# A decoder layer whose branch and output projections take seven block products for eight, in one stream of units with the MLP

## The chip, the cores and the metric

The kernel runs on 1 core of one Trainium2 chip. The metric is the device time in microseconds, the median of three runs. Everything is computed in float32; a product of two float32 matrices is made of three passes on TensorE (below), and the kernel is written in a tile language that places the semaphores and orders the instructions of each engine by a plan of its own, except where the code fixes their order.

## What is computed

One layer: a mixer with three branches, gates, an output projection with a residual, and a squared-ReLU MLP with a residual. D is 1024, the sequence 1024, the MLP's width 4096. The reference, cut to what matters here:

```python
h = rms_norm(x, norm_mix_g)
proj = h @ w_in                        # q, k, v and gates of three branches
y_m = ...                              # mLSTM, 4 heads (branch M)
y_d = ...                              # differential attention, 8 heads (branch D)
y_c = ...                              # cross attention into 256 memory tokens (branch C)
g_m, g_d, g_c = split(sigmoid(h @ w_gate + b_gate), 3)
merged = g_m * (y_m @ w_proj_m) + g_d * (y_d @ w_proj_d) + g_c * (y_c @ w_proj_c)
x = x + merged @ w_out
h2 = rms_norm(x, norm_mlp_g)
x = x + square(relu(h2 @ w_up)) @ w_down
```

## The kernel before, in words

**Three passes.** Each float32 operand is split into a high part (a cast to fp32r, on ScalarE, ACT) and a low part (the difference, on VectorE, DVE): `split2` and `split`, L102 to L115. `mm3` (L117, its matmuls are L91) then multiplies high by high, high by low and low by high into one PSUM bank. Activations lie feature-major: 128 features on the partitions, 1024 positions along the free dimension, cut in two halves of 512.

**Stages.** `run` (L1616) goes through: the norm and transposition of x; branch C; branch M; 64 positions of gate products; branch D; 96 positions of gate products; then `tail`. A position is one `yield` of a generator, mostly three matmuls of 128x512. In branches M and C, `weave` (L476) runs a stream of such positions and fires helper steps at listed positions; in branch D `fill` (L975) draws positions between the steps of attention. The branch outputs y and the gates go to DRAM.

**The tail before.** `tail` (L1297) takes the branches in the order C, M, D. For each, `k_tiles` (L1263) loads the eight y tiles from DRAM and splits them; `load_w` loads and splits the weights of 256 output columns; `group` computes two output tiles by two halves, eight blocks of k each, three passes: 8 x 8 blocks x 2 halves x 3 matmuls a projection. `merge` (L1339) multiplies the PSUM result with the gate fetched from DRAM and adds the three branches; the sum over the third branch is split at once into the operands of the output projection (`hi` and `lo`, which stay in SBUF). The output projection is a `group` of the same kind, with `res` (L1357) as its end: residual, store of x1, a square for the norm, a scaled copy h2, stored to DRAM.

**The MLP before** already works with seven products for eight (Winograd's form of Strassen's scheme): a unit is a quad of 2 x 2 blocks of 128 output features by two halves; a step is one pair of k blocks, seven products of three matmuls (21 matmuls of 128x512); a unit of the up projection has four steps and seven PSUM banks, which rotate over the eight. Four sums of weight blocks (`wino_s`, L1142, on GpSimd, POOL) and four of x blocks (`wino_t`, L1123, three on DVE and one on POOL) make the operands, which are then split; `combine` (L1193) makes four output tiles from the seven banks by seven DVE adds and one ACT copy. `wino` (L1174) begins with the first unit cut in two runs of two steps and its partial sums parked in SBUF, while the remaining x tiles arrive. The norm of the MLP (`rstd`, L1411) is folded in behind the up products: a matmul with ones sums the squares, POOL takes the power -1/2, DVE scales eight identity blocks, and TensorE broadcasts them. `use_up` (L1397) scales, applies ReLU and square, and writes r to DRAM with its four sums. `down` (L1445) makes 16 passes of four steps with 28 accumulators in SBUF; its x tiles come from DRAM and are split again.

**Order.** The MLP and the branches pin the order of TensorE and DVE to that of the program (`InOrder`, L57, and `pin`, L86); ACT, POOL and the DMA queue of SyncE (SP) are ordered by the planner. An engine works its queue strictly in order, so an instruction that waits holds up what stands behind it.

## Time and profile before

| | |
|---|---|
| median of 3 runs | 2211.47 us (2211.36 to 2213.92) |
| profiled execution | 2213.57 us, span 2211.8 us, granted clock 0.995 |
| TensorE busy (matmul) | 2163.4 us, 98% of the span |
| DVE, ACT, POOL busy | 1361.4, 980.7, 527.8 us |
| DMA | 273.06 MB, mean 123 GB/s |
| first and last matmul on kt (branch projections) | start at 1218.5 and 1482.2 us |
| first matmuls of the up and of the down part | 1575.2 and 1891.8 us |

How to read it: the span runs from the first to the last instruction on the core. A row of a group gives line, engine, operation, output and inputs with their shape, the count, then the busy time in us, the mean duration in ns, and the idle time of the engine just before with what ended it. A row of a stretch gives begin and end, its length, and for each engine the busy time with the count of instructions, then TensorE's granted clock, the share of DMA time and GB/s. Matmuls overlap in the pipeline, so the mean duration of one is more than its share of time.

### The profile page before, as it was taken

The page shows a single profiled execution, that of the slowest core. Times are in us where ns is not written, and L with a number is a line of the kernel's source. Part 1 is how long each engine was busy: PE and PEld are TensorE (multiplying, and loading weights), DVE is VectorE, ACT ScalarE, POOL GpSimd, SP SyncE. Part 2 cuts the span into 40 slices and gives each one's busy share as a digit, 9 for nine tenths or more (in the row PEclk, how much of TensorE's full clock was granted, in tenths as well). Part 3 has the DMA queues.
Part 4 walks back from the last instruction along what each step waited for, and adds up shares of the span by engine and source line. Part 5 has one row for each costly group of instructions (what it writes and reads, how often), then busy time and mean ns, then how long its engine had stood idle before and what let it go on. Part 6 is the DMA issues. An engine that isn't in the chain of part 4 may idle for free.

```text
span 2211.8 us, 30588 instructions
## 1 busy us (share of the span) xinstructions
PE 2163.4 (98%) x11097; PEld 1860.7 (84%) x11097; DVE 1361.4 (62%) x2598; ACT 980.7 (44%) x1962; POOL 527.8 (24%) x696
## 2 busy tenths in 40 slices
PE   7999999999999999999999999999999999899999
PEld 5878888898899999999888888877787888688887
DVE  6643575565237777777641232544688877767779
ACT  6543355454336666666542120223444444543332
POOL 2100000000011111111000003202557655565553
PEclk9999999999999999999999999999999999999999
DMA  7023122121333333333343443436435444854444
GB/s 250 29 81 115 50 91 76 44 82 39 107 109 86 93 84 84 88 92 86 101 148 114 134 142 126 138 110 205 147 115 198 159 147 147 318 196 146 145 145 170
DMA packets 127948, 273.06 MB, mean 123 GB/s; under 512 B 12945, under 2 KB 21430, under 8 KB 125750
## 3 DMA queue, kind: packets, MB, share of 16 engines
q1 hardware_dynamic: 125494, 258.53, 37.2%
q10 hardware_dynamic: 2304, 12.58, 1.4%
q8 instruction: 87, 1.43, 0.3%
q14 instruction: 63, 0.52, 0.1%
HBM read 178.76 MB, written 67.14 MB: 111 GB/s over the span
## 4 chain that ended last, share of the span: by engine, by line
PE 77%; DVE 9%; DMA 6%; ACT 4%; issue 2%; POOL 2%; SPq 0%; DVEq 0%; ACTq 0%; POOLq 0%
PE mm L91 46%; PE p L91 20%; PE sc L91 6%; PE tp L94 2%; PE po L91 2%; DVE acc L67 1%; DMA kraw<-y 1%; DMA xr<-h_d 1%; DVE wo L67 1%; DMA y<-yd 1%; DVE u L67 1%; DVE w L112 1%; DMA wraw<-in_wup 0%; DVE xts L67 0%; DVE c L67 0%
## 5 line engine op out<-in xcount | busy, mean ns | idle before, releaser
L91 PE MATMUL mm<-w,hT 128*128 128x384 f32 (+3 forms) x2496 | 473.4, 332 | 8.3 <-DVE dsg L112 5.4
L91 PE MATMUL mm<-hT,w 128*128 128x512 f32 x1920 | 465.7, 395 | 0.0
L91 PEld LDWEIGHTS mm<-hT,w 128*128 128x128 f32 x1920 | 353.5, 188 | 74.2
L91 PEld LDWEIGHTS mm<-w,hT 128*128 128x128 f32 x2496 | 389.2, 190 | 22.2 <-DVE dsg L112 7.6
L91 PE MATMUL p<-xd,wo 128*128 128x512 f32 x1344 | 310.0, 393 | 5.7 <-DVE c L67 2.2
L91 PE MATMUL p<-xo,wo 128*128 128x512 f32 x1344 | 308.2, 390 | 5.7 <-DVE st L1418 2.6
L91 PEld LDWEIGHTS p<-xd,wo 128*128 128x128 f32 x1344 | 253.8, 189 | 61.7 <-DVE c L67 3.3
L91 PEld LDWEIGHTS p<-xo,wo 128*128 128x128 f32 x1344 | 251.0, 188 | 61.5 <-DVE u L67 3.7
L91 PE MATMUL mm<-kt,w 128*128 128x512 f32 x1152 | 262.2, 389 | 1.9 <-ACT w L111 1.1
L112 DVE TENSOR_TENSOR w<-raw,w 128x256 fp32r<-128x256 f32 (+3 forms) x304 | 173.0, 590 | 137.9 <-ACT w L111 136.8
L91 PEld LDWEIGHTS mm<-kt,w 128*128 128x128 f32 x1152 | 216.0, 188 | 47.9 <-ACT w L111 1.5
L111 ACT CAST w<-raw 128x256 fp32r<-128x256 f32 (+3 forms) x304 | 154.3, 530 | 178.9 <-PE mm L91 114.5
L104 ACT CAST wo<-wraw 128x896 fp32r<-128x896 f32 x122 | 115.0, 945 | 208.9 <-PE p L91 115.2
L67 DVE TENSOR_TENSOR wo<-wraw,wo 128x896 fp32r<-128x896 f32 x122 | 143.7, 1195 | 59.4 <-ACT wo L104 59.4
L1145 POOL TENSOR_TENSOR wraw<-wraw 128x128 f32<-128x128 f32 x128 | 97.3, 760 | 245.8 <-DMA wraw<-in_wdown 108.1
L1007 ACT ACTIVATE dpe<-sc,dst,drr 128x256 f32<-128x256 f32 (+7 forms) x128 | 106.7, 834 | 99.7 <-DVE dst L1003 92.0
L999 DVE CUSTOM_DVE_ANT_0 sc<-sc,tmask 128x256 f32<-128x256 f32 (+7 forms) x128 | 97.0, 758 | 12.6 <-PE sc L91 12.5
L127 POOL TENSOR_SCALAR hss<-hss 128x4 f32<-128x4 f32 x8 | 3.3, 410 | 415.4 <-ACT mscr L752 272.9
L91 PE MATMUL sc<-dk,dq 128*128 128x512 f32 (+3 forms) x384 | 90.4, 343 | 0.0
L1148 POOL TENSOR_TENSOR wraw<-wraw 128x128 f32<-128x128 f32 x128 | 85.6, 669 | 10.0
L1146 POOL TENSOR_TENSOR wraw<-wraw 128x128 f32<-128x128 f32 x128 | 87.3, 682 | 0.0
L1147 POOL TENSOR_TENSOR wraw<-wraw 128x128 f32<-128x128 f32 x128 | 87.2, 682 | 0.0
(283 smaller groups left out, 2832.6 us busy)
## 6 DMA issues: line engine op xcount, KB each, us to landing
dk<-dsg SPq DMA_DIRECT2D x64, 256.0 KB, 4.4
wraw<-in_wup SPq DMA_DIRECT2D x64, 256.0 KB, 3.4
r_d<-xts SPq DMA_DIRECT2D x16, 1024.0 KB, 4.1
wraw<-in_wdown SPq DMA_DIRECT2D x64, 256.0 KB, 3.1
xd<-r_d SPq DMA_DIRECT2D x19, 768.0 KB, 7.4
xd<-r_d SPq DMA_DIRECT2D x14, 1024.0 KB, 6.8
raw<-in_wgate SPq DMA_DIRECT2D x48, 256.0 KB, 3.2
gates<-gt SPq DMA_DIRECT2D x48, 256.0 KB, 2.0
```

Of the source, the lines that this page charges most:

```text
L67: return self.tc.keep_in_program_order(f(*a, **k))
L91: self.pin(self.nc.tensor.matmul(out, l, r, start=start, stop=stop))
L94: self.pin(self.nc.tensor.transpose(out, x, self.ident))
L104: self.A.copy(hi, src)
L111: nc.scalar.copy(hi, src)
L112: nc.vector.tensor_sub(lo, src, f32(hi))
L999: V.tensor_tensor_reduce(out=sc[:, 0:n], in0=sc[:, 0:n], in1=self.tmask[:, D - n : D], scale=1.0, scalar=-3.0e38, op0=ALU.add, op1=ALU.max ...
L1007: nc.scalar.activation(pe[c][:, 0:n], sc[:, 0:n], AF.Exp, bias=t8[:, 2 + c : 3 + c], scale=rr[:, i, c : c + 1], accum_out=t8[:, 4 + c : 5 ...
L1145: G.tensor_add(r[:, 4], r[:, 0], r[:, 3])
L1146: G.tensor_sub(r[:, 5], r[:, 4], r[:, 1])
L1147: G.tensor_sub(r[:, 6], r[:, 1], r[:, 0])
L1148: G.tensor_sub(r[:, 7], r[:, 2], r[:, 5])
```

## The change

All four projections get the seven-product form, with the weights packed as quads like those of the MLP; and the four projections, the up and the down part become one program of 128 + 64 steps (`stream`), over one set of x tiles, weight tiles and PSUM banks. The order of units is C, M, D, O (the output projection) with four each, then 16 of up, then 16 passes of down.

- The sums of the projections' weights are made early: `w_jobs` loads half a weight block (64 columns), makes the four sums on POOL and stores seven blocks to DRAM, 128 times, one eighth of a job at each position of branches M and D (`tick`). In the stream, a projection step loads the seven blocks and splits them, high part on ACT, low part on POOL.
- The sums of y are made by `x_jobs` on DVE: C and M under the 64 gate positions, D under the 96; they go to DRAM too. Of the stream's first operands, three x tiles and two weight tiles are loaded and two splits of each x tile done under the 96 positions (`s_early`).
- The sum of the gated branches, and h2 of two of four units, go from their SBUF tiles directly into operands (`x_direct`); the other two of h2 go by DRAM.
- In up, all four x sums are on DVE; the first unit is no longer cut in two, and `rstd` gets the steps 67 and 68 (the fourth of the first and the first of the second up unit) for its parts on TensorE. x tiles of down are loaded from step 114, the down part begins at step 128.
- Loads, splits and ends are listed by step (`at`), and each step's list is issued behind its matmuls (`side`).

The core of the diff:

```diff
     def weave(...)
...
             pos += 1
+            next(self.tick, None)
...
-    PROD = ((0, 0), (1, 2), (4, 4), (5, 5), (2, 6), (3, 3), (6, 1))
+    PROD = ((1, 0), (2, 2), (5, 5), (0, 3), (3, 6), (4, 4), (6, 1))
+    SETS = "CMDO"
+    SLOT = {"C": (0, 1, 2, 3), "M": (4, 0, 1, 2), "D": (3, 4, 0, 1), "O": (2, 3, 4, 0), "U": (1, 2, 3, 0)}
...
+    def wino_t(self, b, t, V):
+        G = self.nc.gpsimd
+        V.tensor_sub(t[:, 1], b[:, 0], b[:, 1])
+        V.tensor_sub(t[:, 0], b[:, 2], b[:, 0])
+        V.tensor_sub(t[:, 2], b[:, 2], t[:, 1])
+        V.tensor_sub(t[:, 3], b[:, 3], t[:, 2])
+
+    def w_jobs(self, pool):
...
+        def load(i):
+            n, s, g, kp, h = jobs[i]
+            r = tiles[i] = pool.tile([P, 7, 64], F32, tag="wj", name=self.name("wj"))
+            nc.sync.dma_start(r[:, 0:4], self.a[self.WNAME[s]][g][:, kp, :, h * 64 : (h + 1) * 64])
+        def store(i):
+            n, h = jobs[i][0], jobs[i][4]
+            nc.sync.dma_start(self.wcd[n][:, :, h * 64 : (h + 1) * 64], tiles.pop(i))
+        load(0)
+        for i in range(len(jobs)):
+            if i:
+                store(i - 1)
+            self.wino_s(tiles[i])
+            for _ in range(4):
+                yield
+            if i + 1 < len(jobs):
+                load(i + 1)
+            for _ in range(4):
+                yield
+        store(len(jobs) - 1)
+
+    def x_jobs(self, pool, jobs, n, period):
+        for s, kp in jobs:
+            for c in range(0, 512, n):
+                r = pool.tile([P, 4, n], F32, tag="xj", name=self.name("xj"))
+                for k in range(2):
+                    src = self.yd[self.YOF[s]][2 * kp + k].rearrange("p (h n) -> p h n", h=2)
+                    nc.sync.dma_start(r[:, 2 * k : 2 * k + 2], src[:, :, c : c + n])
+                for _ in range(period - 4):
+                    yield
+                self.wino_t(r, r, nc.vector)
+                for _ in range(4):
+                    yield
+                nc.sync.dma_start(self.xtd[s][kp][:, :, c : c + n], r)
...
+    def w_split(self, m):
+        if m < 64:
+            t = self.W[m]
+            self.A.copy(t[:, 0], f32(t[:, 1]))
+            self.nc.gpsimd.tensor_sub(t[:, 1], f32(t[:, 1]), f32(t[:, 0]))
+        else:
+            t = self.wo_tile(m)
+            self.split2(t[:, 0], t[:, 1], self.wraw.pop(m))
...
+    def x_direct(self, s, kp, b):
+        t = self.x_tile((s, kp), self.SLOT[s][kp])
+        self.split2(t[:, 0, 0:3], t[:, 1, 0:3], b[:, 1:4])
+        self.wino_t(b, b, self.V)
+        self.split2(t[:, 0, 3:7], t[:, 1, 3:7], b)
...
+        def side(n, use=None):
+            if n + 3 < len(self.seq):
+                self.w_split(n + 3)
+            if n + 4 < 64:
+                self.w_load(n + 4)
+            if 64 <= n + 6 < len(self.seq):
+                self.w_load(n + 6)
+            if use:
+                use()
+            for f in todo.pop(n, []):
+                f()
...
+        def use_gate(s, u, cs):
...
+            for i in (1, 3, 2, 0):
+                V.scalar_tensor_tensor(out=o[:, i], in0=t[:, i], scalar=1.0, in1=cs[i], op0=ALU.add, op1=ALU.mult)
+                if s != "C":
+                    (V if (s, u) == ("D", 3) else G).tensor_add(mg[u][:, i], mg[u][:, i], t[:, i])
...
+        mid = {(67, 2): rs.send, (68, 2): rs.send, (68, 6): rs.send}
...
+        for si, s in enumerate("CMD"):
+            for u in range(4):
+                at(si * 16 + u * 4 + 1, fetch, s, u)
+        for n0, s in ((0, "M"), (16, "D")):
+            at(n0 + 5, self.x_load, s, 0)
+            at(n0 + 7, self.x_split, s, 0)
+            for k in (1, 2, 3):
+                at(n0 + 11 + k, self.x_load, s, k)
+                at(n0 + 13 + k, self.x_split, s, k)
+        for k, n in enumerate((37, 44, 45, 48)):
+            at(n, lambda k: self.x_direct("O", k, mg[k]), k)
+        at(48, open_tail)
+        for u, n in enumerate((49, 53, 57, 61)):
+            at(n, fetch_x, u)
+        at(53, lambda: self.x_direct("U", 0, S["b"]))
+        at(56, h_store, 1)
+        at(60, h_store, 2)
+        at(60, self.x_load, "U", 1)
+        at(62, self.x_split, "U", 1)
+        at(61, self.x_load, "U", 2)
+        at(63, self.x_split, "U", 2)
+        at(63, lambda: self.x_direct("U", 3, S["b"]))
+        for u in range(16):
+            at(68 + 4 * u + 2 * (u == 0), up_rest, u)
+        at(114, self.x_load, "N", 0)
...
     def run(self):
...
+                self.tick = self.w_jobs(cw.enter_context(tc.tile_pool(name="wj", bufs=2, side="right")))
...
+                        jobs = self.x_jobs(xj, [("C", k) for k in range(4)] + [("M", k) for k in (3, 2, 1, 0)], 512, 8)
                         for _ in range(2 * 32):
+                            next(jobs, None)
                             next(self.gates)
...
-            self.tail()
+            self.stream()
```

720 lines of the change are left out of this document (305 added, 415 removed).

## The prediction

> **What bounds the kernel now.** I read the page's table of engines first, then its costliest groups, then the engines' busy time by stretch of the span (us and instruction count of each engine; then granted clock, DMA share, GB/s).
>
> ```profile
> span 2211.8 us, 30588 instructions
> ...
> PE 2163.4 (98%) x11097; PEld 1860.7 (84%) x11097; DVE 1361.4 (62%) x2598; ACT 980.7 (44%) x1962; POOL 527.8 (24%) x696
> ...
> L91 PE MATMUL mm<-kt,w 128*128 128x512 f32 x1152 | 262.2, 389 | 1.9 <-ACT w L111 1.1
> ```
>
> ```profile
> core 0: us, PE busy (x) PEld busy (x) DVE busy (x) ACT busy (x) POOL busy (x), PEclk, DMA share, GB/s
> 245.00:580.00 335.00, 334.39 (x1949) 292.33 (x1948) 184.43 (x464) 159.25 (x436) 12.21 (x16) 1.00 0.21 66
> 760.00:880.00 120.00, 118.17 (x765) 113.93 (x764) 93.12 (x270) 74.81 (x190) 17.25 (x16) 1.00 0.37 89
> 1390.00:1482.00 92.00, 90.40 (x398) 74.23 (x397) 52.22 (x63) 25.20 (x31) 8.68 (x14) 1.00 0.41 132
> 1482.00:1565.00 83.00, 79.26 (x343) 64.86 (x342) 35.35 (x34) 29.79 (x38) 21.51 (x17) 0.98 0.55 179
> 1565.00:1600.00 35.00, 32.38 (x151) 26.81 (x150) 21.24 (x24) 18.86 (x23) 23.12 (x25) 1.00 0.50 171
> 1600.00:1700.00 100.00, 96.92 (x427) 77.64 (x427) 88.27 (x103) 45.08 (x69) 64.66 (x84) 1.00 0.44 155
> 1700.00:1885.00 185.00, 185.00 (x818) 153.19 (x817) 149.03 (x179) 83.45 (x127) 114.20 (x162) 1.00 0.44 153
> 1885.00:1925.00 40.00, 34.33 (x130) 25.80 (x129) 30.99 (x32) 25.86 (x28) 20.26 (x25) 0.87 0.88 329
> 2160.00:2212.00 52.00, 47.47 (x210) 38.81 (x208) 47.35 (x55) 14.75 (x13) 17.68 (x30) 1.00 0.46 164
> ```
>
> TensorE is busy in 98% of the span; no other engine comes near. So the time is the number of matmuls times their pitch, plus what TensorE loses at the seams. The pitch comes from the undisturbed stretch 1700 to 1885 us: 185.00 / 818 = 0.2262 us. (The 389 ns "mean of one" overlaps its neighbours and isn't the price.) The kt row shows the three branch projections, 1152 matmuls; the output projection adds 384 by the code.
>
> The seams show where the stretch is longer than its PE busy column: 1.6 us at 1390, 3.7 at 1482 (branch to output projection), 2.6 at 1565 (output projection to MLP), 3.1 at 1600, 5.7 at 1885 (up to down). At two of them the granted clock falls too (PEclk column): 0.02 of 79 us is 1.6, and 0.13 of 34 us is 4.5. Together 22.8 us. The 4.5 us in the last row are the adds and stores after the last matmul, which stay as they are.
>
> The profiled execution took 2213.57 us for a span of 2211.8, 1.8 us around it; the median of the runs is 2211.47, 0.1% lower. I add the change of span to the median.
>
> **The products.** The four projections are 4 x 8 x 8 blocks x 2 halves x 3 passes = 1536 matmuls of 128x512. With seven products they are 64 steps of 21 = 1344, the shape that the MLP uses. 192 x 0.2262 = **43.4 us** go, all from the bounding engine. A step lasts 21 x 0.2262 = 4.75 us, a unit of four steps 19.0.
>
> **What the products need is paid elsewhere.** These rows price it: groups by shape of DVE and ACT after 1100 us and of POOL in the whole span (busy us, mean ns), and DMA issues (KB, median us to landing).
>
> ```profile
> L67 DVE TENSOR_TENSOR wo<-wraw,wo 128x896 fp32r<-128x896 f32 x122 | 143.7, 1195 | 59.4 <-ACT wo L104 59.4
> L67 DVE TENSOR_TENSOR acc<-acc,p 128x512 f32<-128x512 f32 x100 | 67.4, 686 | 8.3 <-PE p L91 7.5
> ...
> L67 DVE TENSOR_TENSOR xts<-rq,xts 128x512 f32<-128x512 f32 x32 | 36.7, 1146 | 1.1
> L67 DVE TENSOR_TENSOR xd<-xd 128x2048 fp32r<-128x2048 f32 x12 | 29.2, 2436 | 0.0
> ...
> L67 DVE TENSOR_TENSOR xd<-xd 128x1536 fp32r<-128x1536 f32 x16 | 28.8, 1799 | 0.0
> ...
> L1349 DVE TENSOR_TENSOR gl<-mg,gl 128x512 f32<-128x512 f32 x16 | 11.3, 708 | 0.5
> ```
>
> ```profile
> L104 ACT CAST wo<-wraw 128x896 fp32r<-128x896 f32 x122 | 115.0, 945 | 208.9 <-PE p L91 115.2 <-POOL wraw L1148 36.6 <-DVE acc L67 17.6
> ...
> L104 ACT CAST xd<-xd 128x1536 fp32r<-128x1536 f32 x16 | 23.7, 1480 | 15.9 <-DMA xd<-r_d 15.9
> L104 ACT CAST xd<-xd 128x2048 fp32r<-128x2048 f32 x12 | 22.9, 1912 | 48.0 <-DMA xd<-r_d 48.0
> ```
>
> ```profile
> L1146 POOL TENSOR_TENSOR wraw<-wraw 128x128 f32<-128x128 f32 x128 | 87.3, 682 | 0.0
> ...
> L1368 POOL TENSOR_TENSOR ssq<-ssq,sq 128x512 f32<-128x512 f32 x14 | 20.9, 1503 | 111.5 <-ACT sq L1367 111.5
> L1347 POOL TENSOR_TENSOR mg<-mg,gl 128x512 f32<-128x512 f32 x16 | 20.5, 1287 | 156.0 <-DVE gl L1345 156.0
> ...
> L127 POOL TENSOR_SCALAR hss<-hss 128x4 f32<-128x4 f32 x8 | 3.3, 410 | 415.4 <-ACT mscr L752 272.9 <-DVE w L112 142.5
> ...
> L128 POOL TENSOR_TENSOR st<-st,mhalf 128x8 f32<-128x8 f32 x1 | 1.7, 1652 | 0.1
> ```
>
> ```profile
> raw<-in_wgate SPq DMA_DIRECT2D x48, 256.0 KB, 3.2
> gates<-gt SPq DMA_DIRECT2D x48, 256.0 KB, 2.0
> ...
> wib<-g_dwi SPq DMA_DIRECT2D x8, 256.0 KB, 3.4
> ```
>
> *Within a projection unit* the work is hidden. DVE: seven PSUM combines at 0.69 us and four gate products at about 0.7 are 7.6 us of 19.0; each x tile split adds 1.80 + 2.44. ACT: four weight casts (0.945) and a copy, 4.4 us. POOL has no row for the 128x896 difference that it takes over from DVE; between its 128x128 (0.68) and 128x512 (1.29 to 1.50) the slope is 1.6 to 2.1 ns an element, so 1.9 to 2.4 us; four of them and four adds of mg are 13 to 16 us of 19.0. Without that cover it would bound the unit.
>
> *Gates to the first unit.* W2, X[C,3] and W3 are loaded only when the stream begins, into space that I take to be hT's, so behind the last gate matmul. That is 2.75 MB; at the 329 GB/s of the row at 1885, 8.4 us, then casts and differences of 5 to 6 us, against three steps (14.3 us). Cover just holds: 1 us, bounds 0 to 4.
>
> *C to M, M to D.* Three x tiles of 1.84 MB are fetched in consecutive steps behind a 0.46 MB weight load each and a 1.05 MB gate load: 8.4 MB, 25.5 us at 329 GB/s. The third is wanted six steps (28.5 us) after its burst begins, with 1.48 + 1.80 us or more of splitting ahead. ACT and SP are the queues held meanwhile: the cast for a late weight blocks what follows. 2 us each, bounds 0 to 6.
>
> *D to O.* mg[3] goes straight into operands: gate product and add (6 us), difference 1.80, transform about 3.5, cast 1.91, difference 2.44, some 16 us behind the last D matmul, against 14.3 plus two products (1.4). 1.5 us, bounds 0 to 4.
>
> *O to U* is where I expect the largest new loss, on DVE's queue, whose order is fixed by hand. From the end of step 62 to the second difference of W67 it holds: split of U1 4.24, combine of the last O unit 4.8, W65 and W66 2.4, residual 2.8, split of U2 4.24, then for U3 difference 1.80, transform 4 x 1.15 = 4.6, difference 2.44, then W67 1.2: 28.5 us. PE wants W67 four steps later, at 19.0 + 0.45. That is 9.1 us late, about 2 more where DVE waits for ACT's casts between. Then rstd, which by the code has three steps between its first PE part and the scaled identities today and gets one (4.75 us): POOL 0.41 + 1.65 behind up to four sums of 0.68, and scaled identities on DVE; 2 us. A clock loss as in the row at 1885, 2. Sum 15, bounds 5 (DVE gets ahead in step 62) to 24 (each cast serial, clock as at 1885). POOL, with differences and next weight sums together in steps 58 to 60, runs a few us late under it.
>
> *Within U* the fourth transform moves from POOL to DVE, 16 x 1.15 us over 305 us: busy share 149/185 = 0.81 becomes 0.87, as in the row at 1600 (0.88, 3.1 us idle). 3 us, bounds 1 to 10. *U to down*: x tiles come up to five steps early: 1 us, bounds 0 to 6.
>
> Seams after: 1 + 4 + 1.5 + 15 + 3 + 1 = **25.5 us** (bounds 6 to 60) in place of 22.8: **+2.7**.
>
> **What is moved under M, gates and D.** 128 half jobs on weights: a load, four POOL sums of 128x64, a store, in turns of eight stream positions. A sum lies between 0.41 (128x4 row) and 0.68: 1.6 to 2.7 us a job, while POOL is busy 12 of 335 us in M and 17 of 120 in D (stretches 245 and 760). Their price is indirect: POOL's rsqrt for M and D, and SP's y and operand transfers, queue behind a job that waits for its data, DVE's fixed order behind the rsqrt. There TensorE idles 0.6 us in 335 (first row of the stretches) and 1.8 in 120 (second), so there is slack to lose. The two engines also meet: an add with both operands in SBUF takes DVE 0.708 us where POOL is nearly idle (L1349) and 1.146 where it runs wraw sums (xts), the same shape. D has by the code 192 such DVE instructions (64 weight differences, 64 combinations of maps, 64 scalings of keys); if all met POOL, 192 x 0.44 = 84 us over some 500, and DVE's share would go from 93/120 = 0.78 to 0.94; POOL's new share is about a third, so 0.83: not the bound. 2 us, bounds 0 to 15. By the Trainium skill, SBUF — State Buffer (Who interferes with whom), such a DVE instruction and a GpSimd one that reads SBUF exclude each other for a whole instruction. The two rows agree with that; by it alone, with POOL always first, this term would stand at its upper bound, 15. The 64 gate positions (43.4 us) also take eight x jobs of 2.1 MB plus 4.2 MB of gate weights and stores: 21 MB, 64 us at 329 GB/s. The overhang of 20 us runs into D, and if DVE's transforms that wait for it stand ahead of D's first weight splits, TensorE waits too. 4 us, bounds 0 to 20. The D jobs, three C tiles and the last gates are 21 MB too, in 96 positions (65 us): at the limit, but nothing wants the last of it before step 21, so nothing is charged. Together **+6** (bounds 0 to 35).
>
> **Sum**: -43.4 + 2.7 + 6 = **-34.7 us; 2211.47 - 34.7 = 2176.8 us**.
>
> **Rivals.** *The stream closes the seams*: loads and splits come early enough, O to U costs its lower bound. For it: operands are loaded steps ahead, and 1700 to 1885 shows a stream without any idle. Against it: the DVE count above. -43.4 - 22.8 + 10 = -56: 2155 us.
>
> *The seams and the overhang cost near their upper halves*: O to U 22, bursts 5 each, the rest as above: seams 38.5; overhang 15, prepared work 18; -43.4 + 15.7 + 18 = -9.7: 2202 us. For it: DVE's fixed order passes on any late load. Against: ACT and SP may be reordered ahead of waiting work.
>
> *The prepared weights hold up M and D*, and the kernel is slower. A buffer's turn is a load (2 to 3.2 us), four sums (2.7), a store (2.0 by the gates row) = 7 to 8 us, and two buffers share two periods of eight positions, 2 x 8 x 0.68 = 11 us. From a store of about 6 us the turn is longer than its time; each further us costs 0.5 us a job, 64 in all, of which I let half reach TensorE through POOL's wait. At 7.1 us the gain is eaten; at 8 the time is 2176.8 + 64 = 2241 us. For it: rows of 64 columns, 256 bytes, 128 x 7 of them in a store. Against: 256 KB read in 512-byte runs (wib) lands in 3.4 us, in 2 KB runs (raw<-in_wgate) in 3.2. By the Trainium skill, DMA: Bandwidth & Descriptors (Specifications), a transfer below 512 B doesn't reach line rate because the DMA engine then reads, modifies and writes; no run here shows a 256-byte write. By that rule every store of a job would be a dear one, and this rival the likely case.
>
> **How the numbers follow.** The forecast (2165 to 2190) gets 0.57, closed seams 0.18, dear seams 0.17, held-up branches 0.08. A measurement of this kernel can tell about 0.2% (4.4 us) from no change. Of the dear seams 0.03 lies within that, of the last rival 0.01: faster 0.89, same 0.04, slower 0.07. The range 2154 to 2204 leaves out the last rival, the dear seams' upper third and the lowest quarter of the closed ones, about 0.18.
>
> **What would show it.** 4032 matmuls after the gates at a pitch of 0.226 us; a stretch without idle inside the C, M, D units; TensorE waiting for DVE (x or wo tiles, the adds of combine) in the four steps after the last O matmul, 8 to 15 us, and the clock below 1 there; no idle at the turn to down; the last 4.5 us unchanged; the D stretch as long as before within 10 us, with PE waiting, if at all, for D's first weight splits. Wrong: an idle PE inside the projection units (POOL or DMA bounds them), or M and D longer by more than the projections' gain.

## The result, and the profile after

The changed kernel takes **2397.15 us** (median of 4 runs, 2394.73 to 2404.76) against 2212.69 for the kernel before on the same chip (4 runs): a ratio of **1.084, 95% interval 1.0813 to 1.0866**. I had forecast 2176.8, faster; it is 184 us slower. The profiled execution took 2395.46 us, its span is 2393.6.

One thing of what stands on record above is wrong and must be put right first. I wrote all four sums of `wino_t` as DVE's. In the code only three are; the second, `t[:, 0]`, is POOL's, in `x_direct`, `h_store`, `up_rest` and `x_jobs` alike (L1142). So nothing moved from POOL to DVE in up, and I charged for it; and I missed that DVE, whose order in the stream is fixed, stands still inside each transform until POOL's queue comes to that one sum.

The page after, its engines and the groups that are new:

```profile
span 2393.6 us, 31611 instructions
...
PE 2198.1 (92%) x10905; PEld 1858.9 (78%) x10905; DVE 1493.7 (62%) x2705; ACT 1028.6 (43%) x1991; POOL 903.1 (38%) x1304
...
L92 PE MATMUL p<-xo,wo 128*128 128x512 f32 x4032 | 967.7, 401 | 88.2 <-DVE c L67 19.5
...
L1226 POOL TENSOR_TENSOR wo<-wo 128x896 fp32r<-128x896 f32 x64 | 161.0, 2525 | 121.9 <-ACT wo L1225 115.5
...
L1133 POOL TENSOR_TENSOR wj<-wj 128x64 f32<-128x64 f32 x128 | 49.9, 390 | 317.1 <-DMA wj<-in_wpm 93.3
```

TensorE has 192 matmuls fewer (10905 for 11097), and its share fell from 98 to 92%: the time went into idle TensorE. Its 4032 matmuls of the stream alone have 88 us of idle before them, and POOL's first sum of a weight job (L1133) stood waiting 317 us. By stretch of the span (columns as in the prediction's table of stretches):

```profile
core 0: us, PE busy (x) PEld busy (x) DVE busy (x) ACT busy (x) POOL busy (x), PEclk, DMA share, GB/s
217.00:600.00 383.00, 344.03 (x1878) 295.17 (x1879) 197.28 (x493) 152.72 (x422) 136.64 (x352) 0.93 0.59 141
640.00:721.00 81.00, 59.33 (x261) 47.12 (x259) 21.79 (x40) 13.68 (x30) 12.66 (x12) 0.91 0.77 274
1326.00:1604.00 278.00, 247.66 (x1012) 194.34 (x1011) 167.35 (x153) 85.38 (x81) 171.72 (x79) 0.95 0.54 191
1604.00:1719.00 115.00, 88.32 (x337) 67.50 (x336) 69.88 (x72) 46.28 (x55) 64.39 (x43) 0.85 0.50 177
1719.00:1800.00 81.00, 59.78 (x239) 47.27 (x238) 56.64 (x67) 31.14 (x40) 34.51 (x48) 0.85 0.38 131
1800.00:2000.00 200.00, 200.00 (x875) 164.10 (x875) 155.24 (x186) 91.21 (x138) 123.86 (x179) 1.00 0.44 156
2062.00:2100.00 38.00, 26.30 (x97) 18.61 (x96) 29.78 (x28) 21.51 (x25) 21.52 (x25) 0.89 0.88 327
```

The rows are most of branch M, its end with the gates ahead of branch D, the 48 steps of C, M and D, the output projection, the entry into up, steady up, the entry into down. Only steady up runs as I took the whole stream to run. Every other row has idle TensorE, and with it a granted clock below 1. In the first row 39 us are idle, and a clock of 0.93 over 344 us is 24 more: 63 us.

Stage by stage, from the starts of the first matmuls of each in the two traces:

| stage | before, us | after, us | difference |
|---|---|---|---|
| up to branch M | 200.5 | 216.9 | +16.4 |
| M and the 64 gates, up to D's first 128x384 matmul | 419.3 | 504.2 | +84.9 |
| D and the 96 gates | 598.7 | 605.3 | +6.6 |
| projections of C, M, D | 263.9 | 277.5 | +13.6 |
| output projection | 92.8 | 115.2 | +22.4 |
| up | 316.6 | 343.5 | +26.9 |
| down and end | 320.0 | 331.0 | +11.0 |

They add up to +181.8, the difference of the spans. So 108 us were lost ahead of the stream, where I had put 6, and 74 in it, where I had put a gain of 41.

**Ahead of the stream.** POOL's waits in branch M (total us, times, longest us), then one place in POOL's timeline (start, us, then in brackets the idle time before and what ended it):

```profile
POOL wj L1133 <- DMA wj<-in_wpd: 81.4, 22, 8.0
POOL wj L1133 <- DMA wj<-in_wout: 73.9, 28, 7.4
POOL wj L1133 <- DMA wj<-in_wpm: 66.6, 17, 11.1
POOL hss L128 <- ACT mscr L754: 0.4, 2, 0.2
```

```profile
306.37 0.32 POOL L1135 TENSOR_TENSOR wj<-wj 128x64 f32<-128x64 f32 x1
314.31 0.32 POOL L1133 TENSOR_TENSOR wj<-wj 128x64 f32<-128x64 f32 x1 [7.62 <-DMA wj<-in_wpm]
314.72 0.19 POOL L128 TENSOR_SCALAR hss<-hss 128x4 f32<-128x4 f32 x1
```

The jobs don't go in turns of eight positions, as listed. The planner, free to order POOL and SP, put them as early as two buffers let it: all their sums lie between 45 and 583 us, under C and M. POOL is either summing or waiting for the next job's load, and M's inverse roots (hss) stand behind that. That is what my rival of the held-up branches said one would see.

SP's queue is held as well. Its waits between 217 and 600 us (L1159 is a job's store, L1155 its load), then the chain that ended last in this stretch, as shares by line, before and after:

```profile
SPq L1159 <- POOL wj L1135: 65.0, 47, 2.5
SPq L1155 <- DMA wc_d<-wj: 60.6, 53, 2.9
SPq L1159 <- POOL wj L1133: 40.1, 20, 3.8
```

```profile
by line: PE mm L91 82.4%; PE sc L91 8.2%; PE tp L94 2.7%; PE tp L91 2.4%; DMA ngb<-g_dng 1.5%; DMA g_dng<-g_c 0.4%; DVE ks L115 0.4%; ACT ks L114 0.4%; ACT ngb L700 0.3%; DVE mpT L112 0.2%; DVE ngb L693 0.2%; ACT mpT L111 0.2%; DVE ngb L711
by line: DMA wc_d<-wj 18.8%; PE mm L92 18.1%; DMA wj<-in_wpd 12.1%; DMA wj<-in_wout 6.2%; issue 5.6%; DMA wj<-in_wpm 4.0%; DMA ngb<-g_dng 3.4%; POOL wj L1133 3.4%; POOL wj L1134 3.2%; POOL wj L1135 3.0%; POOL wj L1136 2.7%; DMA y<-ym 2.5%; 
```

Before, the chain through M is TensorE's work. After, 53% of it is the jobs' own round: a store lands, the next load goes into that buffer, POOL sums, SP stores. The chain is inferred from semaphores, but it says where M's work hangs on the jobs: six times a transfer that SP issues behind a job's load or store, and twice an inverse root on POOL. One of the six (start, us):

```profile
425.20 0.47 POOL wj L1135
...
425.68 0.51 SPq L1159
...
426.25 3.18 DMA y<-ym
...
429.53 0.72 ACT ym L773
```

The store of a job waits for its last sum; M's store of its output y (`y<-ym`) stands behind it in SP's queue; ACT waits for that to land.

Behind M, the x jobs reach past the gates. Waits between 640 and 725 us:

```profile
POOL xj L1142 <- DMA xj<-y: 51.3, 6, 15.7
...
PE mm L92 <- ACT w L112: 21.4, 3, 17.9
```

**In the stream.** A step should take 4.75 us. The dear ones, by the starts of their first matmuls (step: us): 1 to 3: 10.3, 10.8, 10.5; 18: 10.1; 28: 10.6; 34: 13.6; 40: 8.1; 48: 24.8; 51: 13.6; 56: 10.9; 64: 12.4; 66: 9.0; 67: 22.4; 68: 9.5; 128 to 132: 41.2 together. Step 48 is the first of the output projection. DVE's timeline there:

```profile
1590.42 3.48 DVE L67 SCALAR_TENSOR_TENSOR gtile<-gtile,u 128x512 f32<-128x512 f32 x2
1593.83 2.85 DVE L67 TENSOR_TENSOR xo<-mg,xo 128x1536 fp32r<-128x1536 f32 x1
1596.71 2.50 DVE L67 TENSOR_TENSOR mg<-mg 128x512 f32<-128x512 f32 x1
1601.65 3.32 DVE L67 TENSOR_TENSOR mg<-mg 128x512 f32<-128x512 f32 x2 [2.44 <-POOL mg L1142]
1606.99 5.84 DVE L67 TENSOR_TENSOR xo<-mg,xo 128x2048 fp32r<-128x2048 f32 x2 [2.02 <-ACT xo L105]
1612.87 0.69 DVE L67 TENSOR_TENSOR mg<-mg 128x512 f32<-128x512 f32 x1
1615.00 3.27 DVE L67 TENSOR_TENSOR mg<-mg 128x512 f32<-128x512 f32 x2 [1.44 <-POOL mg L1142]
1620.29 2.29 DVE L67 TENSOR_TENSOR xo<-mg,xo 128x2048 fp32r<-128x2048 f32 x1 [2.02 <-ACT xo L105]
1622.49 0.68 DVE L67 TENSOR_TENSOR c<-u,p 128x512 f32<-128x512 f32 x1
```

The last line is the combine of D's last unit, whose matmuls ended at 1604. It frees the PSUM banks that the next products want. Ahead of it stand the direct tiles for the second and third merged pair, listed at positions 44 and 45: split, transform, split, twice, with a wait for POOL or ACT in each.

### The profile page after: what moved, and what is told of

Same layout as the page of the kernel before. It is cut to its first block, busy times and chain, and to the rows that moved or that the text cites. A ratio compares the mean times of both kernels' runs of the same rounds, so it can differ in the third digit from the quotient of the medians.

```text
span 2393.6 us, 31611 instructions
## 1 busy us (share of the span) xinstructions
PE 2198.1 (92%) x10905; PEld 1858.9 (78%) x10905; DVE 1493.7 (62%) x2705; ACT 1028.6 (43%) x1991; POOL 903.1 (38%) x1304
## 2 busy tenths in 40 slices
DMA packets 310087, 365.95 MB, mean 153 GB/s; under 512 B 197505, under 2 KB 214182, under 8 KB 302118
## 4 chain that ended last, share of the span: by engine, by line
PE 53%; DMA 19%; DVE 10%; POOL 8%; issue 5%; ACT 4%; SPq 1%; DVEq 0%; POOLq 0%; ACTq 0%
PE p L92 27%; PE mm L92 18%; DMA wc_d<-wj 4%; PE sc L92 4%; PE po L92 2%; DMA xj<-y 2%; DMA wj<-in_wpd 2%; DVE xo L67 2%; DMA wj<-in_wpc 2%; PE tp L95 1%; DVE u L67 1%; POOL mg L1329 1%; DMA xtD_d<-xj 1%; DMA wj<-in_wpm 1%; POOL wo L1226 1%
## 5 line engine op out<-in xcount | busy, mean ns | idle before, releaser
L92 PE MATMUL p<-xo,wo 128*128 128x512 f32 x4032 | 967.7, 401 | 88.2 <-DVE c L67 19.5
L92 PEld LDWEIGHTS p<-xo,wo 128*128 128x128 f32 x4032 | 770.5, 192 | 283.8 <-DVE c L67 24.9
L1226 POOL TENSOR_TENSOR wo<-wo 128x896 fp32r<-128x896 f32 x64 | 161.0, 2525 | 121.9 <-ACT wo L1225 115.5
L1133 POOL TENSOR_TENSOR wraw<-wraw 128x128 f32<-128x128 f32 x128 | 94.1, 735 | 287.1 <-DMA wraw<-in_wdown 109.7
L1133 POOL TENSOR_TENSOR wj<-wj 128x64 f32<-128x64 f32 x128 | 49.9, 390 | 317.1 <-DMA wj<-in_wpm 93.3
L67 DVE TENSOR_TENSOR xo<-xo 128x1536 fp32r<-128x1536 f32 (+1 forms) x60 | 145.3, 2439 | 26.9 <-ACT xo L105 26.9
L105 ACT CAST xo<-xo 128x1536 fp32r<-128x1536 f32 (+1 forms) x60 | 101.6, 1695 | 81.6 <-DMA xo<-r_d 55.7
L67 DVE TENSOR_TENSOR u<-u,p 128x512 f32<-128x512 f32 x160 | 107.0, 686 | 15.9 <-PE p L92 3.2
L1225 ACT CAST wo<-wo 128x896 fp32r<-128x896 f32 x64 | 59.5, 939 | 131.2 <-DMA wo<-wc_d 123.5
L1002 DVE CUSTOM_DVE_ANT_0 sc<-sc,tmask 128x256 f32<-128x256 f32 (+7 forms) x128 | 97.0, 757 | 12.6 <-PE sc L92 12.5
L67 DVE TENSOR_TENSOR c<-u,p 128x512 f32<-128x512 f32 x64 | 43.9, 686 | 85.2 <-ACT u L1413 56.8
```

Source lines behind the costliest of these rows:

```text
L67: return self.tc.keep_in_program_order(f(*a, **k))
L92: self.pin(self.nc.tensor.matmul(out, l, r, start=start, stop=stop))
L105: self.A.copy(hi, src)
L1002: V.tensor_tensor_reduce(out=sc[:, 0:n], in0=sc[:, 0:n], in1=self.tmask[:, D - n : D], scale=1.0, scalar=-3.0e38, op0=ALU.add, op1=ALU.max ...
L1133: G.tensor_add(r[:, 4], r[:, 0], r[:, 3])
L1225: self.A.copy(t[:, 0], f32(t[:, 1]))
```

## The experiments

A run changes the changed kernel unless said otherwise. Times are compared with its profiled execution, 2395.46 us. The kernel before took 2212.0 to 2216.4 us (single runs, or the median of one job) beside them, so a difference under 5 us isn't read; the changed kernel's own four runs lie 10 us apart, so differences of 7 to 15 us rest on the stages that the traces show, and less on the time alone. A diff shows the core of its edit; `...` stands for lines left out.

**1. No weight jobs.**

```diff
-                self.tick = self.w_jobs(cw.enter_context(tc.tile_pool(name="wj", bufs=2, side="right")))
+                self.tick = iter(())
...
-            self.nc.sync.dma_start(f32(t[:, 1]), self.wcd[self.SETS.index(s) * 16 + u * 4 + k])
+            self.nc.sync.dma_start(f32(t[:, 1]), self.yd[2][m % 8][:, 0:896].rearrange("p (q n) -> p q n", q=7))
```

> This kernel is the changed one without the 128 weight jobs: no load, no sum and no store of them runs anywhere; in the stream the weights of branch and output projections are loaded, in tiles of the same size and rows of the same length, from branch C's stored output instead of from the prepared copy, so the products are of other numbers. Theory (the jobs, which the trace shows between 20 and 600 us, under branches C and M, cost these two branches 16 and 62 us): branch M falls from 437 us to 375-385, the projections start 70-80 us earlier than at 1326, their stream is as long as in the changed kernel, time 2315-2330. Rival (C and M became slower for another reason, such as the order in which the planner now lists their work, or branch M's x jobs): M stays over 420 and the time over 2375.

Measured: 2316.22 us, **79 less**. M begins at 200.9 us and the projections at 1245 instead of 1326; the stream is the same to 2 us. Branch M is as before the change:

```profile
201.00:577.00 376.00, 374.06 (x2199) 327.85 (x2200) 211.47 (x554) 175.41 (x480) 12.22 (x16) 1.00 0.23 68
```

**2. Whole rows.** What of a job is dear? First the short rows, my own mechanism for the slower case.

```diff
-                r = tiles[i] = pool.tile([P, 7, 64], F32, tag="wj", name=self.name("wj"))
+                r = tiles[i] = pool.tile([P, 7, P], F32, tag="wj", name=self.name("wj"))
...
-            nc.sync.dma_start(self.wcd[n][:, :, h * 64 : (h + 1) * 64], tiles.pop(i))
+            nc.sync.dma_start(self.wcd[jobs[i][0]], tiles.pop(i))
...
```

> The same weight jobs in 64 pieces of 128 columns with one buffer, instead of 128 pieces of 64 columns with two: the same bytes and the same POOL sums over the same elements, but rows of 2 KB and 3.5 KB, so no packet of 256 bytes from the jobs. If the short rows are the price of the jobs (the mechanism of my slower case), branch M comes down from 437 us to 375-400 and the time to 2325-2350. If it is the POOL sums (its queue, or the port that DVE and POOL share) or only where the transfers stand in SP's order, M stays at 415-440 and the time over 2370.

Measured: 2422.06 us, 27 **more**. Packets under 512 bytes fall from 197505 to 15234 and the DMA share in M from 0.59 to 0.43, and M is no faster: TensorE is busy less still.

```profile
217.00:600.00 383.00, 319.08 (x1740) 274.73 (x1739) 186.72 (x463) 141.29 (x390) 94.82 (x180) 0.92 0.43 139
```

So taking the short rows away buys nothing. The run alone doesn't clear them, since the job's tile is twice as wide and there is one buffer where there were two: POOL waits longer for the loads (253 us in this stretch, against 222). Run 3, with the same short rows and two buffers, does.

**3. The transfers without the sums.**

```diff
...
-            self.wino_s(tiles[i])
...
```

> The same weight jobs with the same loads and stores, but the four POOL sums of each left out (the three added blocks are zeros, block 0 is the weight's own, so the products are of other numbers); two tiles stand for the pool's two buffers. If the sums are the price (POOL's queue, or the port it shares with DVE), branch M comes down from 437 us to 375-400 and the time to 2325-2350. If the transfers are, M stays at 415-440 and the time over 2370; the jobs, now free of the sums, can then even turn faster and the DMA share in C and M rise over 0.6.

Measured: 2335.40 us, **60 less**, with the same bytes and the same packets. POOL's sums on 128 half blocks are three quarters of the jobs' price; all their transfers together, short rows and all, make up the other 19 us (against run 1). With the sums gone POOL's queue is free, and no store waits for a sum in SP's queue: the run doesn't tell the two apart.

```profile
202.00:575.00 373.00, 358.67 (x2105) 312.39 (x2106) 206.98 (x542) 168.96 (x466) 11.00 (x14) 1.00 0.59 146
```

**4. Sums that can't wait.**

```diff
...
-            self.wino_s(tiles[i])
+            self.wino_s(two[1])
...
```

> The weight jobs with all their loads, stores and as many POOL sums of the same shape, but the sums read and write a tile of their own that no load fills, and the loads and stores go round through one other tile whose three added blocks are zeros (the products are of other numbers). So POOL's work and its use of the port stay, and what it can wait for is gone. If the price of the sums is that POOL stands waiting for a load at the head of its queue (220 us of such waits in the changed kernel between 217 and 600 us) while branch M's short POOL work queues behind it, branch M is 375-405 us as in the run without sums and the time 2320-2350. If it is POOL's time, or DVE slowed on the shared port, M stays over 420 us and the time over 2370.

Measured: 2466.95 us, 71 more: a miss of both theories. Free of loads, all 512 sums were placed in the first 200 us, and branch C's own POOL steps stood behind them. M began at 328 us instead of 217, and then ran as in run 3 (460 us to D's first matmul, against 458). In C, POOL's waits for loads aren't needed for the harm; a POOL queue that is full for any reason does it. The stretches of C, and who waited:

```profile
0.00:100.00 100.00, 29.56 (x108) 21.82 (x109) 23.55 (x48) 24.68 (x39) 85.59 (x262) 0.70 0.34 118
100.00:217.00 117.00, 59.99 (x267) 48.18 (x267) 39.95 (x61) 35.24 (x66) 97.86 (x292) 0.74 0.27 65
```

```profile
DVE xk L234 <- POOL r L129: 64.7, 8, 19.1
```

DVE is busy a quarter to a third of these stretches, so it isn't a shared port that slows it; it waits for an inverse root that POOL hasn't come to.

**5. POOL kept in the listed order**, as I had assumed it.

```diff
...
-        g = self.nc.gpsimd
+        g = self.G
...
-            self.wino_s(tiles[i])
+            self.wino_s(tiles[i], self.G)
```

The first pair of lines is in `rsqrt_mean`, which makes every branch's inverse roots. `self.G` is POOL kept in the order of the program, as `self.V` is DVE.

> The changed kernel with one thing added: POOL's weight-job sums and the two POOL steps of every inverse root keep, among themselves, the order in which the program lists them (as DVE's stream does), so the jobs go in turns of eight stream positions, 71 of them under branch M and 56 under D, as I had assumed, in place of nearly all under C and M. Loads, stores and work are the same. Theory (dear is the density: sums queued as fast as two buffers turn, each job's first sum waiting for its load in front of the branches' short POOL steps): branch C is back to 200 us, M at 385-415 us instead of 437, D 0-20 longer, time 2330-2370. Rival (a job's sums cost a branch about as much wherever they lie, 62 us for 128 jobs, since every one waits for its load at the head of POOL's queue): M about 405-415 and D 25-35 longer, time 2380-2410.

Measured: 2381.61 us, 14 less: the rival's time. The stretch up to M is 203.8 us, 13 less; M and the gates take 487.8, 16 less; D takes 14 more (456.1 us between its first and last 128x384 matmul, against 442.4), which is the theory's range (0 to 20) and not the rival's (25 to 35). In M the price of a job is the same: M alone loses 43 us with 56 jobs' sums in it, where it lost 62 with 85. There the number counts, not the density; in C and D a job costs less. Spread out, a first sum still waits for its load nearly every time (line 67 is the helper that keeps the order):

```profile
POOL wj L67 <- DMA wj<-in_wpd: 70.4, 13, 15.0
POOL wj L67 <- DMA wj<-in_wpc: 62.6, 18, 6.6
```

**6. No x jobs of C and M ahead of D; 7. none of D's ahead of the stream.**

```diff
...
-                        jobs = self.x_jobs(xj, [("C", k) for k in range(4)] + [("M", k) for k in (3, 2, 1, 0)], 512, 8)
+                        jobs = iter(())
...
-                        jobs = self.x_jobs(xj, [("D", k) for k in range(4)], 256, 12)
+                        jobs = iter(())
```

> The eight x jobs of branches C and M, listed under the gates before branch D, are left out; the stream loads the branch outputs themselves in the place of their four sums (same tiles, the same bytes in packets of the same length or longer, other numbers). Theory (the jobs overhang the gates and hold D's first weight splits, 23 us): the stretch from M's last transpose to D's first 128x384 matmul falls from 67 us to 44-47, time 2372-2380; steps 1 to 3 of the stream, which lose 16 us behind a POOL queue that waits for branch D's x jobs, stay as they are. Rival (D's first matmul waits because the DMA engines are full of weight jobs' transfers): the stretch falls by less than 10 us, time over 2385.

> The changed kernel without the transforms of branch D ahead of the stream (they are listed under the last 96 gate matmuls); D's products read D's output itself in the place of the four sums, so they are of other numbers. Theory (these jobs' sums wait on POOL for loads, and the first projection weights' low differences stand behind them in POOL's queue, so steps 1 to 3 of the stream lose 17 us): these three steps fall from 31.5 us to 14.5-18, time 2379-2386. Rival (the first weights and tiles of C come late by themselves, or wait for ACT): the three steps stay over 26 us, time over 2390.

Measured: 2374.19 us (**21 less**) for the first line, 2380.40 (**15 less**) for the second: both in the expected range. In the first, TensorE has no gap from 640 us to D's first matmul at 701:

```profile
640.00:701.00 61.00, 61.00 (x276) 49.94 (x275) 12.34 (x30) 18.23 (x40) 2.45 (x4) 1.00 0.34 110
```

In the second, steps 1 to 3 take 18.2 us instead of 31.5 (14.5 to 18 expected). DVE and POOL had stood waiting for y to be read back, with the first splits behind.

**8. The weights' low differences on DVE.**

```diff
-            self.nc.gpsimd.tensor_sub(t[:, 1], f32(t[:, 1]), f32(t[:, 0]))
+            (self.V if self.pinned else self.nc.vector).tensor_sub(t[:, 1], f32(t[:, 1]), f32(t[:, 0]))
```

> In the changed kernel the low differences of the 64 projection weights go from POOL (62 of 2.52 us in the stream) to DVE (about 1.0-1.2 us each, as DVE's own 128x896 differences take). Nothing else is changed. Theory (POOL's long differences stretch DVE's work on the shared port: 3.47 us for a 128x2048 difference against 2.3-2.4, 1.64 for a gate against 0.68; and they hold the adds into mg and PE itself, 8.8 us): the losses in the 48 steps of C, M and D fall from 50 us to 20-35 and those of O from 39 to 25-35, time 2350-2382. Rival (DVE's fixed order is the bound, and 1.1 us more in each step makes it worse): time 2395-2430.

Measured: 2384.80 us, 11 less, outside the theory's range. A difference takes 1.23 us on DVE where POOL took 2.52, and the 128x2048 split differences fall from 2.79 us to 2.46; but only O gains clearly (its loss 39 to 33), and C, M and D stay at 49, where the theory had 20 to 35. POOL's share in the stream's loss is small.

**9. The transforms' second sum on DVE.**

```diff
...
-        self.wino_t(b, b, self.V)
+        self.wino_t(b, b, self.V, self.V)
...
```

> In the changed kernel the second sum of each transform made in the stream for O and for up goes from POOL to DVE, so that DVE never waits in the middle of a transform for POOL's queue (17 us of such waits between 1326 and 1790 us). Nothing else is changed; branch C's, M's and D's transforms listed ahead of the stream keep theirs. Theory (these waits sit on the path into O and into up): the losses of O and of steps 64 to 71 fall by 8-20 us together, time 2375-2388. Rival (DVE's order would make the same steps late anyway, and it now has eight sums of 0.7 us more): within 4 us of the changed kernel, 2391-2400.

Measured: 2394.76 us: no difference, the rival. The 5 us that O gains are given back in C, M and down. The wait that I had overlooked in `wino_t` is real (17 us on DVE) and costs nothing that can be measured.

**10. The second and third direct tile left out.**

```diff
-            at(n, lambda k: self.x_direct("O", k, mg[k]), k)
+            if k in (1, 2):
+                at(n, lambda k: self.X.update({("O", k): self.X["O", 0]}), k)
+            else:
+                at(n, lambda k: self.x_direct("O", k, mg[k]), k)
...
```

> In the changed kernel the direct splits and transforms of the second and third merged pair (listed at stream positions 44 and 45, ahead of the combine of branch D's last unit in DVE's order) are left out; O's products take the first pair's tile in their place, and the fourth pair's in O's last unit (so the output is of other numbers, and the fourth tile of up comes free one step later). Theory (these two blocks of DVE work keep the combine waiting and with it PE, 20 us at step 48): step 48 falls from 24.8 us to 5-11, the loss of O by 14-20, time 2374-2382. Rival (the gates' adds, or the weights' differences on POOL, hold the combine just as long): step 48 stays over 17 us, time over 2388.

Measured: 2377.30 us, **18 less**, and step 48 takes 7.2 us instead of 24.8: the place that the timeline above shows.

**11. DVE's order left to the planner in the stream.**

```diff
+        self.V = nc.vector
         V, A, G = self.V, self.A, nc.gpsimd
```

> The changed kernel with one thing less: in the stream DVE's instructions are no longer kept in the order in which the program lists them; the planner places them as it does elsewhere. The work is the same. Theory (the stalls at the seams come from DVE work that is listed ahead of a combine, or that stands ahead of one while it waits itself): the losses at steps 48, 64 to 68 and 128 to 132 (20, 34 and 17 us) fall together by 25-45 us, time 2350-2372. Rival (at the seams DVE simply has more work than the steps last, in whatever order): the same losses within 10 us, time 2385-2405; a planner that puts the combine late in a steady step could make it slower than that.

Measured: 2371.96 us, **24 less**, at the upper end of the theory's time, but not where it said: steps 48, 64 to 68 and 128 to 132 fall by 5.8, 1.0 and 5.7 us, 12.5 together where 25 to 45 were expected; 7 more are M's steps. Order counts, but at the seams it isn't the most of the loss, and at the entry into up next to nothing.

**12. Up's second to fourth tile left out at the seam; 13. no low differences of M's and D's x tiles.**

```diff
...
-        at(56, h_store, 1)
-        at(60, h_store, 2)
-        at(60, self.x_load, "U", 1)
-        at(62, self.x_split, "U", 1)
-        at(61, self.x_load, "U", 2)
-        at(63, self.x_split, "U", 2)
-        at(63, lambda: self.x_direct("U", 3, S["b"]))
+        for k in (1, 2, 3):
+            at(60, lambda k: self.X.update({("U", k): self.X["U", 0]}), k)
...
```

```diff
-            (split or self.split2)(t[:, 0, c], t[:, 1, c], f32(t[:, 1, c]))
+            if s in "MD":
+                self.A.copy(t[:, 0, c], f32(t[:, 1, c]))
+            else:
+                (split or self.split2)(t[:, 0, c], t[:, 1, c], f32(t[:, 1, c]))
```

> In the changed kernel the second to fourth tile of up's operand are left out at the seam: no stores, loads, transforms and splits of them under the output projection (up's products take the first tile in their place until step 103 to 111, when tiles loaded in the steady stretch replace them; other numbers). Theory (the entry into up waits for DVE, which has these transforms and splits in front of O's last combines and of up's first weights): steps 64 to 68 fall from 72 us to 26-40, time 2360-2378. Rival (the entry waits for the combines themselves, the squares on POOL and the chain of the normalization): steps 64 to 68 stay over 55 us, time over 2380.

> In the changed kernel the low differences of M's and D's x tiles, 16 pieces of DVE work of 2.6 and 3.5 us, are left out (the low half of these operands then holds the value itself, so other numbers). All loads and ACT's high halves stay. Theory (what holds PE at steps 16 to 44 is the amount of DVE work that falls together where one branch's products end and the next one's tiles are split): the losses of M's and D's steps fall from 31.5 us to 5-15, time 2377-2390. Rival (the tiles' loads, 1.8 MB each into a slot that comes free one step at a time, or the low differences of the weights on POOL): the losses stay over 24 us, time over 2388.

Measured for 12: 2388.02 us. Steps 64 to 68 fall from 58.1 us (not 72, as I had added them up) to 37.9, but the time by 7 only, since the tiles split later cost the steady stretch about 11. What is left is step 68, 16.8 us: by DVE's order the combine of up's first unit stands behind the chain of the norm (sum on PE, POOL, eight scaled identities); this is read from the listing, and no run takes the chain away. Measured for 13: 2377.87 us, **18 less**, M's and D's losses 14 instead of 31.5: the amount of DVE work where one branch ends and the next one's tiles are split, not the loads.

**14. Runs 1, 6, 7, 10, 12 and 13 in one kernel.**

> The edits of five runs in one kernel: no weight jobs (weights from branch C's output), no x jobs of C, M and D, no direct tiles for O's second and third pair, no second to fourth tile at up's entry, no low differences of M's and D's x tiles. If the terms simply add up: 2395 less 81, 23, 15, 18, and less what the two runs beside this one give (20-35 and 5-18 by their theories): 2205-2233. If one of these works covers another (two that wait for the same engine), less comes back than the sum and the time is over 2245.

Measured: 2233.15 us, 162 less. The six single gains are 79.2, 21.3, 15.1, 18.2, 7.4 and 17.6, together 158.8. **The terms add up.** And with this work missing (three tiles of up are still loaded and split late, which costs the steady stretch 9 us), the kernel is still about 19 us slower than the one before.

**15 to 17. The change arranged otherwise:** no jobs, raw weights into the stream, POOL's sums there, every other sum and difference of the projections on DVE, x jobs under M and D.

```diff
-            self.nc.sync.dma_start(f32(t[:, 1]), self.wcd[self.SETS.index(s) * 16 + u * 4 + k])
+        r = self.wraw[m] = self.wrs[max(m - 1, 0) % 3].tile([P, 7, P], F32, tag="wraw", name=self.name("wraw"))
+        src = self.a[{"U": "wup", "N": "wdown"}.get(s) or self.WNAME[s]][u]
+        self.nc.sync.dma_start(r[:, 0:4], src[:, k % 16])
+        self.wino_s(r)
...
```

> The change with its preparation laid out otherwise, computing the same as the reference. No weight jobs: each projection weight's raw four blocks are loaded in the stream into a tile of its own, POOL adds the three sums and the difference there and the split's low part is on DVE, as up and down have it all along (three split buffers instead of four up to O). Branch C's transforms are listed under branch M and M's under D, in pieces of 128 columns, D's under the last gates with two buffers, and all sums of every transform for C, M, D, O and up are on DVE. By the runs so far: 2395 less 81 (no jobs), less 23 (no x jobs ahead of D), less 0-17 (POOL's queue free at the stream's start), less 0-11 (low differences on DVE), and 0-25 back for x jobs that stand on DVE in M and D waiting for their loads: 2265-2315, likeliest 2280, so still slower than the kernel before. If POOL's sums in the stream do not keep up, the steps of C, M and D are over 4.9 us throughout and the time is over 2330.

Measured: 2318.22 us, 3 outside the range. The stream begins at 1239 us instead of 1326, as hoped, but D's steps then lose 33 us instead of 16: DVE is full there.

> The arrangement with raw weights in the stream (2318 us, computing the same as the reference) with DVE's order in the stream left to the planner, as in the run that took 23 us from the changed kernel. If the two gains add up: 2285-2305. If the planner has less to gain here because DVE, with the weights' low differences and all transform sums on it, is simply full at the seams: 2308-2325.

Measured: **2282.28 us**, better than either case and the fastest of the arrangements: with DVE full, its order is worth 36 us instead of 24.

> The rearranged version with DVE's order left to the planner (2282 us, computing the same as the reference), with two more changes. Branch C's transforms are listed under branch D too, behind which M's already cost nothing that its profile shows (D's matmuls 440 us there and in the kernel before), instead of under branch M. And the normalization chain at up's entry (the sum of squares on PE, two steps on POOL, eight DVE products, eight transposing matmuls) is put one step and more later into PE's order, behind the combine of up's first unit, which stood 12 us behind it in the run without up's tiles. If both are what held the kernel: 14 us less before the stream, 6-12 less at steps 67 to 71, time 2254-2268. If the chain only moves the stall to the step where it now stands: 2264-2275. Either way slower than the kernel before, by 1.8 to 2.8%.

Measured: 2296.74 us (4 runs, 2294.86 to 2299.51), 1.0366 times the kernel before (1.0344 to 1.0387), slower than run 16 and a miss of both theories. M is the hoped-for 14 us shorter; but D, which hid M's x jobs, doesn't hide C's as well and is 30 us longer; and the chain only moves its stall (up's loss 38 us, as in run 16). The two rows are M with the gates, and D:

```profile
202.00:622.00 420.00, 417.72 (x2386) 364.14 (x2387) 222.98 (x584) 188.24 (x507) 13.44 (x18) 0.99 0.25 77
622.00:1092.00 470.00, 444.05 (x2774) 425.04 (x2773) 351.01 (x1069) 261.73 (x674) 63.53 (x56) 0.99 0.46 118
```

None of the versions beats the kernel before.

## Why the prediction failed, point by point

**The products.** Right: 4032 matmuls and no idle in steady up. Their pitch is 200.00 / 875 = 0.2286 us there, for 0.2262. The shortest steps are as long as before (4.76 us), so it lies in some longer ones; steps 69 to 127 lose 5 us in all, and why wasn't tried.

**"What is moved under M, gates and D: +6 (0 to 35)".** This is the first step that failed; it measured 108. Three sentences of it were wrong. "In turns of eight stream positions": what code lists isn't where a free planner puts it. I had read the list as a schedule (run 5: worth 14 us). "Weight jobs 2 (0 to 15)": 79 us, of which the sums are 60. I had set POOL's busy time (12 of 335 us) against the jobs' and found room; what counted was the order of two queues. Branch C's short POOL steps stand behind the sums, as run 4 shows at its worst. In M the chain runs mostly through SP: M's transfers stand behind a job's store, that behind its sums, these behind the job's load. I had written that POOL's rsqrt and SP's transfers "queue behind a job that waits for its data"; the mechanism was there, and I priced it at next to nothing. The bound of 15 came from DVE slowed beside POOL; the trace has that too, but small: DVE's 128x256 weight differences in M take 0.450 us after, 0.419 before and in run 3. And the x jobs' overhang, "4 (0 to 20)", is 21, with 15 more at steps 1 to 3, where I wrote "nothing wants the last of it before step 21": the data weren't wanted, but POOL's and DVE's queues were.

**"The prepared weights hold up M and D".** The rival that came true, at a chance of 0.08, and by half of its mechanism. The jobs' wait passes on to TensorE, as it said; but its threshold, a store of over 6 us, wasn't what did it: a job's 224 KB store in 256-byte rows lands in 2.8 us (median; the longest traced, 6.0). A buffer's turn is 8.6 us (85 jobs' sums between 217 and 583 us, two buffers), below the 11 that I gave it; but the free order left no 11 us. By the rule that I quoted with it (the Trainium skill, DMA: Bandwidth & Descriptors, Specifications) short rows should be dear. The trace agrees so far that they take more of the DMA engines (share 0.59 at 141 GB/s, 0.43 at 139 with whole rows); the time doesn't hang on it (runs 2 and 3). I had taken a buffer's turn as harmless while it fits its period. A turn that fits still means a wait at the head of the queue, nearly every time.

**"Within a projection unit the work is hidden"; C to M, M to D 2 each; gates to C 1.** 50 us lost in 48 steps, for 5: 17 at steps 1 to 3 (above), and 31.5 in M and D, of which 18 are DVE's low differences of x tiles (run 13). I had counted DVE per unit, 7.6 of 19 us; but the splits of three tiles fall together with a combine and the gate products, in the few steps around a branch's end. POOL's difference is 2.52 us, above my 1.9 to 2.4, and of little weight (run 8). (The bursts of 8.4 MB come to 7.95 by their own terms; nothing hangs on it.)

**"D to O 1.5 (0 to 4)".** Step 48 loses 20 us and the output projection 39 in all. I took the one tile behind the last gate product and left out the two listed ahead of the combine (run 10: 18 us).

**"O to U is where I expect the largest new loss": 15 (5 to 24).** The place and the mechanism (DVE's fixed order) were right, the size was 34, steps 64 to 68. Run 12 gives 20 to the tiles; 12 of the rest are at step 68, where by the listing the chain of the norm stands ahead of a combine in DVE's order; I had put 2.

**"Within U" 3 and "U to down" 1.** The first charged for work that wasn't moved. The steps 128 to 132 lose 17 us: the old seam there, 5.7 us idle and 4.5 of clock, which I had nearly written off, grew. In the free order of run 11 it is 6 us less.

**"Wrong: an idle PE inside the projection units, or M and D longer".** Both happened; these were the right places to look.

What stays open: how much of the sums' 60 us goes through SP's queue in M and how much through POOL's. The chain points to SP, but no run holds one queue free and leaves the other as it is. The direct wait, DVE's hS behind hss, is no measure: 12.1 us between 220 and 570 us, but 9.6 before the change. Of the 19 us that remain in run 14 the place is known and the cause isn't: 7 more than before ahead of the stream, 19 fewer in C, M and D, 4 more in the output projection, 16 in up (9 by the late tiles), 12 in down, where the seam at steps 128 to 132 stands in every run.

## What to carry to other kernels

"Off the critical path" isn't a property of an engine's busy share. Before moving work to an idle engine, name the short steps that the critical chain needs from it, and ask what will stand ahead of them. Ask it of the DMA queue as well: a store that waits for background work holds the critical chain's own transfers. A background instruction that waits for a load holds what stands behind it until the load lands, and where the planner orders the queue, it may be placed much earlier than the listing shows.

In a stream with a fixed order, count an engine's work between the end of one unit and the freeing of its PSUM banks, not per unit on average. A saving of 2% in matmuls doesn't pay for seams that each lose 10 to 20 us.

## What the runs showed of the hardware

Idle TensorE costs twice. In the stretches shown, the granted clock is below 1 wherever TensorE has gaps for a good part: 0.70 with TensorE 30% busy, 0.85 with 77%, 0.93 with 90%, and 1.00 in the stretches without gaps. The share alone doesn't set it: the clock was 0.91 with 73% ahead of branch D and 0.85 with 74% at the entry into up. In branch M it made 24 of 63 us, and without the jobs (run 1) both losses are gone.

With rows of 256 bytes the DMA engines were busy for 0.59 of branch M at 141 GB/s, with whole rows for 0.43 at 139 (run 2). A store of 224 KB in short rows landed in 2.8 us, one of 448 KB in whole rows in 2.5.
